# Two PSUM banks for the gate products, and one block's lookups written behind the second half's norm

## The chip, the cores and the metric

The kernel runs on one core of a Trainium2 chip. The metric is the device time of one execution in microseconds (us). The median of the runs of the kernel before is 4191.13 us. Profiles come from one execution that the hardware profiler recorded; its times are counted from the start of its span.

## What is computed

One layer of a diffusion backbone over 1024 tokens with 1024 channels: token mixers (two linear-attention scans in both directions, merged by gates and followed by an output projection), then a PEER expert feed-forward, then a final normalisation. The change touches the border of the two and the first part of PEER:

```python
x = x + mod[2] * mixer_output(...)                 # output projection w_out, residual
h = modulate(rmsnorm(x, norm_ffn_g), shift, scale) # norm before PEER
q = h @ wq                                         # 8 heads x 2 x 128
v1, i1 = top_k(q1 @ k1.T, 16); v2, i2 = top_k(q2 @ k2.T, 16)
top_s, top_c = top_k(v1[:, None] + v2[None, :], 16)   # 16 experts per head, 128 per token
expert = i1[top_c // 16] * 128 + i2[top_c % 16]       # the lookups
gate = softmax(top_s)
out = sum_e gate[e] * gelu(u[e] . h) * v[e]           # 16384 experts
```

## The kernel before, in words

The 1024 tokens are 8 blocks of 128. The mixers work on two halves of 4 blocks. After them comes, per half, `merge_step` (branch projections, 8 steps), `out_proj` (the output projection, one 128-row tile `xt` per block, two PSUM products `pso` each) and `next_norm` (row statistics on ACT, scaling on DVE at L84 through `norm_T`, transposes on PE into `pt_m`, and the normalised halves `hb`).

While the second half is merged and projected, the first half already chooses its experts. A generator `first()` yields after each piece: `choosing(0, pp)` (scores and top-16 of 8 heads, nine pieces per head) and then `route(n)` for blocks 0, 1 and 2. `route` is the lookup step: it turns the chosen candidate numbers into the two key numbers and the softmax weights (`sel`), almost all on DVE (tiles `abur`, `abfr`, `eqr`, `selr`, L801 to L840). `CS = (9, 1, 1)` says how many pieces are taken from the generator at each merge step, after each projected tile, and in the norm. 8 merge steps times 9 exhaust `choosing`; the projected tiles 0, 1 and 2 then take `route` of blocks 0, 1 and 2, the fourth finds the generator empty, and so does the norm.

PEER is evaluated in two ways. Blocks 0, 1 and 4 gather their expert rows one by one (`gathering`: an indirect DMA issued by POOL at L1000, six rows in flight; a DVE instruction at L979 for rows of `peer_u`, at L984 for rows of `peer_v`). Blocks 2, 3, 5, 6 and 7 go densely over all 16384 experts in 128 tiles of 128, and need a dense gate matrix per block. `gate_block` builds it for four tokens at a time: two DVE instructions make one-hot vectors `oh` (L1068, which the profile names L89, and L1069; four buffers), eight PE matmuls add them up in PSUM as `pgm` (L1070 to L1073), and one ACT instruction evicts the bank into `gs` (L1074), which goes to DRAM after 8 such steps (L1076). There are 160 steps: 64 for blocks 2 and 3, 96 for blocks 5, 6 and 7.

```python
pgm = ppg.tile([P, TB, P], F32, name=f"pgm{n}_{c0}", tag="go")
for t in range(TB):
    for j in (2, 3):
        PE.matmul(pgm[:, t, :], lhsT=oh[:, 0, :, t], rhs=oh[:, j, :, t], start=j == 2, stop=j == 3)
S.activation(gs[:, :, t0:t0 + TB].rearrange("p i n -> p n i"), pgm, AF.Copy, scale=SA / SG)
```

Between the gate steps `early_tile` runs the first product of 75 expert tiles: eight PE transposes of the loaded rows into `put` (L1021), ACT copies the high half into `uT` (L1024) and a full copy into `uf` (L1026), POOL subtracts them for the low half of `uT` (L1027), and 48 matmuls accumulate into `ph` (L100 in `mm3`), which ACT evicts with Gelu into `ac` (L1039). A counter of estimated costs (`U_US`, `G_E`, the numbers that the generators yield) says how many such tiles and gathers are written between the gate steps; the change leaves those numbers as they are. Between blocks 3 and 5 stands `choosing(1)`, the choice for the second half.

PSUM has 8 banks of 2 KB per partition. In this part `put` holds two, the two halves of `ph` one each, `pgm`, the transposes `tr` and the scores `q` one each: seven.

The program text is not the order on the engines. A scheduling layer takes the recorded instructions and lays out one queue per engine, moving an instruction ahead of others written before it where its inputs allow; each engine then runs its queue strictly in order.

Of the kernel before, what the change touches and what calls it, by code (L numbers as in the profile page):

```python
# [8 lines left out]
F32 = mybir.dt.float32  # L9
# [9 lines left out]
P = 128  # L19
# [25 lines left out]
TB = 4  # L45
# [12 lines left out]

U_US = 6.5
G_E = 4.2  # L60
CS = (9, 1, 1)
FILL = (0, 0, 2, 0, 0, 1, 1, 0)
AHEAD = 6
PRE = 0.25
# [3 lines left out]
def tile_layer(ctx: ExitStack, tc: tile.TileContext, x, c, ctxt, c_ctx, ada_w, ada_b, norm_mix_g,  # L68
# [19 lines left out]
    def tt(eng, out, in0, in1, op):  # L88
        eng.tensor_tensor(out=out, in0=in0, in1=in1, op=op)  # L89
# [6 lines left out]
    def mm3(ps, lh, ll, rh, rl, nk=KC):  # L96
        n, last = 0, 3 * nk - 1
        for k in range(nk):
            for a, b in ((lh, rh), (lh, rl), (ll, rh)):
                PE.matmul(ps, lhsT=a(k), rhs=b(k), start=n == 0, stop=n == last)  # L100
                n += 1
# [39 lines left out]
    def rms_cols(tiles, pl, tag):  # L141

        n = len(tiles)
        ss = pl.tile([P, n], F32, name=f"ss_{tag}", tag="ss", bufs=3)
        for i, t in enumerate(tiles):
            sq = pl.tile([P, D], F32, name=f"sq_{tag}{i}", tag="sq")
            S.activation(sq, t, AF.Square, accum_out=ss[:, i:i + 1])
        S.activation(ss, ss, AF.Ln, scale=1.0 / D, bias=eps)
        S.activation(ss, ss, AF.Exp, scale=-0.5)
        return ss  # L150

    def norm_T(tiles, ss, dst, sc, sh, pl, pp, tag, rows_of=None):

        for i, t in enumerate(tiles):
            tsc(V, t, t, ss[:, i:i + 1], ALU.mult)
        w = len(tiles) * P
        for k in range(KC):
            pt = pp.tile([P, 512], F32, name=f"pt_{tag}{k}", tag="pt", bufs=2)
            for i, t in enumerate(tiles):
                PE.transpose(pt[:, i * P:(i + 1) * P], t[:, k * P:(k + 1) * P], ident)  # L160
            hi = dst(0, k)
            S.activation(hi, pt[:, :w], AF.Identity, scale=sc(k), bias=sh(k))
            yt = pl.tile([P, 512], F32, name=f"yt_{tag}{k}", tag="yt", bufs=2)
            tsc(V, yt[:, :w], pt[:, :w], sc(k), ALU.mult, sh(k), ALU.add)
            tt(G, dst(1, k), yt[:, :w], hi, ALU.subtract)
            if rows_of is not None:
                rows_of(k, yt)
# [5 lines left out]
    with ExitStack() as mixers:  # L173
# [704 lines left out]
        def out_proj(hf, yT, fill=None):  # L878
            tiles = []
            for i in range(4):  # L880
                n = hf * 4 + i
                xt = mg.tile([P, D], F32, name=f"xr{n}", tag="xr", bufs=4)
                ld(out=xt, in_=x[n * P:(n + 1) * P, :])
                for h2 in range(2):
                    cs = slice(h2 * 512, (h2 + 1) * 512)
                    ps = pp.tile([P, 512], F32, name=f"pso{n}_{h2}", tag="pj", bufs=2)
                    mm3(ps, lambda k: yT[:, k, 0, i * P:(i + 1) * P], lambda k: yT[:, k, 1, i * P:(i + 1) * P],
                        lambda k: wo[:, 0, k, cs], lambda k: wo[:, 1, k, cs])
                    tm = mg.tile([P, 512], F32, name=f"tm{n}_{h2}", tag="tm")
                    tt(V, tm, ps, mod2[:, cs], ALU.mult)  # L890
                    tt(G, xt[:, cs], xt[:, cs], tm, ALU.add)
                st_(out=x1_d[n * P:(n + 1) * P, :], in_=xt)
                tiles.append(xt)
                if fill is not None:
                    for _ in range(CS[1]):
                        next(fill, None)
            return tiles

        def h2_rows(hf):

            own = [n - hf * 4 for n in GB if n // 4 == hf]
            o = sum(n // 4 < hf for n in GB)

            def rows_of(k, yt):
                pt = pp.tile([P, 512], F32, name=f"ptr{hf}_{k}", tag="tr")
                w = len(own)
                for i, b in enumerate(own):
                    PE.transpose(pt[:, i * P:(i + 1) * P], yt[:, b * P:(b + 1) * P], ident)
                hn = mg.tile([P, 2, P], F32, name=f"hn{hf}_{k}", tag="hn", bufs=2)
                S.activation(hn[:, 0:w], pt[:, 0:w * P].rearrange("p (a b) -> p a b", a=w), AF.Copy, scale=1.0 / SH2)  # L910
                st_(out=h2_d[o:o + w, :, k * P:(k + 1) * P].rearrange("a p b -> p a b"), in_=hn[:, 0:w])

            return rows_of

        def next_norm(hf, tiles, fill=None):
            ss = rms_cols(tiles, mg, f"x1_{hf}")
            if fill is not None:
                for _ in range(CS[2]):
                    next(fill, None)
            norm_T(tiles, ss, lambda s, k: hb[hf][:, s, k, :], lambda k: cols2[:, 1, k:k + 1], lambda k: cols2[:, 0, k:k + 1],  # L920
                   mg, pp, f"m{hf}_", h2_rows(hf))

        yin = load_y(0)
        yT = mg.tile([P, KC, 2, HT], F16, name="yT0", tag="yT")
# [6 lines left out]
        yT = mg.tile([P, KC, 2, HT], F16, name="yT1", tag="yT")  # L931
# [8 lines left out]

        first_half = first()
        for j in range(KC):
            for _ in range(CS[0]):
                next(first_half, None)
            merge_step(1, j, yin, yT)
        next_norm(1, out_proj(1, yT, first_half), first_half)
        for _ in first_half:
            pass
        if "x1" in dbg:
# [94 lines left out]
    with ExitStack() as st:  # L1044
        pg = pool(st, "pg", reuse_waits="tile")
        ppg = pool(st, "ppg", space=PSUM, reuse_waits="tile")
# [14 lines left out]
        def gate_block(rT, n, nb):  # L1061

            gs = pg.tile([P, P, NB], F32, name=f"gs{n}_{nb}", tag="gs", bufs=2)
            for t0 in range(0, NB, TB):
                c0 = nb * NB + t0
                oh = pg.tile([P, 4, P, TB], F16, name=f"oh{n}_{c0}", tag="oh", bufs=4)
                cols_ = lambda j: rT[:, j:j + 2, c0:c0 + TB].unsqueeze(2).to_broadcast([P, 2, P, TB])
                tt(V, oh[:, 0:2], iota.unsqueeze(1).to_broadcast([P, 2, P, TB]), cols_(0), ALU.is_equal)  # L1068
                vmark[0] = V.tensor_tensor(out=oh[:, 2:4], in0=oh[:, 1:2].to_broadcast([P, 2, P, TB]), in1=cols_(2), op=ALU.mult)  # L1069
                pgm = ppg.tile([P, TB, P], F32, name=f"pgm{n}_{c0}", tag="go")  # L1070
                for t in range(TB):
                    for j in (2, 3):
                        PE.matmul(pgm[:, t, :], lhsT=oh[:, 0, :, t], rhs=oh[:, j, :, t], start=j == 2, stop=j == 3)  # L1073
                S.activation(gs[:, :, t0:t0 + TB].rearrange("p i n -> p n i"), pgm, AF.Copy, scale=SA / SG)  # L1074
                yield 1.65
            st_(out=G_d[DB.index(n) * (P // NB) + nb], in_=gs)  # L1076
# [196 lines left out]
```

## Time and profile before

| | |
|---|---|
| median of 3 runs | 4191.13 us (4185.23 to 4202.76) |
| the profiled execution's own time | 4186.54 us |
| its span | 4184.8 us |
| PE busy | 3875.4 us, 93% |
| DVE busy | 2961.0 us, 71% |
| POOL busy | 1624.5 us, 39% |
| ACT busy | 1417.9 us, 34% |
| DMA, mean over the span | 211 GB/s |
| gate products (L1073), first to last start | 1902.2 to 2824.3 us |

Busy shares are averages over stages with different limits, so the rows below are cut by stage: the border to PEER (1860 to 1900 us), the gates of blocks 2 and 3 (1900 to 2140), the choice of the second half without any gate step (2140 to 2440), and the gates of blocks 5, 6 and 7 (2440 to 2826). "Idle" of an engine in such a stretch is the stretch less its busy time.

### The profile page before, as it was taken

The numbers are of one execution on the slowest core, as the hardware profiler recorded it, in microseconds if no ns is written. First come the engines' busy times: TensorE is split into PE (matmuls) and PEld (weight loads), VectorE is DVE, ScalarE is ACT, GpSimd is POOL, SyncE is SP. The second block draws the span as 40 slices with busy tenths as digits, with TensorE's granted clock in tenths as the row PEclk, the third lists the DMA queues.
The fourth block names the chain that finished last, engine by engine and source line by source line (L and its number), as shares of the span: only waits on it lengthen the run. The fifth ranks groups of instructions, "written<-read, shape, count | busy, mean of one in ns | idle before, by whom it ended". The sixth has DMA issues, their size and how long they took to land.

```text
span 4184.8 us, 60506 instructions
## 1 busy us (share of the span) xinstructions
PE 3875.4 (93%) x23802; PEld 2352.4 (56%) x23802; DVE 2961.0 (71%) x5292; ACT 1417.9 (34%) x2186; POOL 1624.5 (39%) x1197
## 2 busy tenths in 40 slices
PE   6999999999999999978999988897999999999997
PEld 2665666656565444436766656675555554554553
DVE  5345446343546513688889899995889898889999
ACT  5335344242333202115532344553222222222222
POOL 2111111010111002016666577765555465555553
PEclk8999999999999999999999999999999999999999
DMA  5222122221323573317887778898999998988997
GB/s 191 73 79 86 46 81 82 63 85 46 91 71 108 162 261 125 116 57 270 328 309 276 248 254 314 307 335 310 310 316 321 314 318 308 323 289 304 319 309 247
DMA packets 435308, 884.66 MB, mean 211 GB/s; under 512 B 28512, under 2 KB 245067, under 8 KB 431439
## 3 DMA queue, kind: packets, MB, share of 16 engines
q0 software_dynamic: 110592, 402.70, 27.7%
q1 hardware_dynamic: 202676, 320.19, 22.8%
q10 hardware_dynamic: 121754, 157.89, 10.8%
q8 instruction: 187, 3.06, 0.3%
q14 instruction: 99, 0.80, 0.1%
HBM read 764.80 MB, written 115.88 MB: 210 GB/s over the span
## 4 chain that ended last, share of the span: by engine, by line
PE 39%; DVE 30%; DMA 10%; issue 10%; ACT 5%; POOL 4%; SPq 0%; ACTq 0%; DVEq 0%; POOLq 0%
DVE gacc L984 7%; DVE row_False L979 4%; PE ph L100 4%; DMA acr<-act_d 3%; DMA row_False<-in_peer_u_dram,idx 3%; PE pj_f0h L100 3%; PE pv_g L100 3%; PE pv_h L100 2%; PE pgm L1073 2%; PE pj_f1h L100 2%; PE pj_m L100 2%; DVE acc L1168 2%; POOL row_False L1000 2%; DVE v L94 2%; PE pq L100 2%
## 5 line engine op out<-in xcount | busy, mean ns | idle before, releaser
L100 PE MATMUL ph<-hb,uT 128*128 128x256 f16 (+1 forms) x6144 | 905.1, 304 | 44.6 <-POOL uT L1027 33.6
L100 PE MATMUL pe<-v,w 128*128 128x512 f16 x3840 | 864.2, 385 | 70.2 <-DVE acc L1168 65.4
L100 PEld LDWEIGHTS <-uT 128*128 128x128 f16 x6144 | 614.0, 100 | 271.1 <-POOL uT L1027 37.4
L100 PEld LDWEIGHTS <-w 128*128 128x128 f16 x3840 | 380.5, 99 | 541.1 <-issue 105.2
L1000 POOL DMA_INDIRECT row_True<-in_peer_v_dram,idx x384 | 482.3, 1256 | 360.2 <-DVE gacc L984 293.4
L1000 POOL DMA_INDIRECT row_False<-in_peer_u_dram,idx x384 | 504.8, 1315 | 267.8 <-DVE row_False L979 174.0
L979 DVE SCALAR_TENSOR_TENSOR row_False<-row_False,h2n 128x1024 f32<-128x1024 f32 x384 | 520.9, 1389 | 70.1 <-DMA row_False<-in_peer_u_dram,idx 60.2
L984 DVE SCALAR_TENSOR_TENSOR gacc<-row_True,dots,gacc 128x1024 f32<-128x1024 f32 x381 | 535.0, 1404 | 22.6 <-DMA row_True<-in_peer_v_dram,idx 21.1
L1027 POOL TENSOR_TENSOR uT<-uf,uT 128x512 f16<-128x512 f32 x256 | 379.3, 1494 | 200.3 <-ACT uf L1026 197.9
L93 ACT ACTIVATE v<-vn 128x1024 f16<-128x1024 f32 x128 | 135.1, 1056 | 495.4 <-DMA vn<-in_peer_v_dram 368.6
L1074 ACT ACTIVATE gs<-pgm 128x512 f32<-128x512 f32 x160 | 171.8, 1074 | 167.2 <-PE pgm L1073 160.1
L94 DVE SCALAR_TENSOR_TENSOR v<-vn,v 128x1024 f16<-128x1024 f32 x128 | 176.5, 1380 | 54.2 <-ACT v L93 54.2
L1073 PE MATMUL pgm<-oh 128*128 128x128 f16 x1280 | 176.7, 295 | 40.4 <-ACT gs L1074 26.3
L1039 ACT ACTIVATE ac<-ph 128x256 f32<-128x256 f32 (+1 forms) x256 | 109.6, 440 | 289.6 <-PE ph L100 258.3
L1168 DVE TENSOR_TENSOR acc<-pe,acc 128x512 f32<-128x512 f32 x310 | 206.6, 683 | 0.8 <-PE pe L100 0.8
L100 PE MATMUL pj_m<-hb,w_m 128*128 128x512 f16 x768 | 182.3, 393 | 2.3 <-DVE lf_g L86 1.6
L1073 PEld LDWEIGHTS <-oh 128*128 128x128 f16 x1280 | 144.9, 116 | 67.6 <-issue 45.5
L100 PE MATMUL pq<-hb,w_wq 128*128 128x512 f16 x768 | 177.1, 384 | 1.0 <-POOL hb L89 0.7
L1024 ACT ACTIVATE uT<-put 128x512 f16<-128x512 f32 x256 | 153.7, 600 | 69.0 <-PE put L1021 61.6
L1026 ACT ACTIVATE uf<-put 128x512 f32<-128x512 f32 x256 | 155.1, 606 | 25.5 <-POOL uT L1027 25.1
L100 PEld LDWEIGHTS <-hb 128*128 128x128 f16 x1536 | 150.3, 98 | 17.7 <-issue 0.3
L89 POOL TENSOR_TENSOR lf_g<-lf_g,ab_g 128x1280 f32<-128x1280 f32 x8 | 23.1, 2890 | 336.3 <-ACT ab_g L639 336.3
(364 smaller groups left out, 5649.8 us busy)
## 6 DMA issues: line engine op xcount, KB each, us to landing
un<-in_peer_u_dram SPq DMA_DIRECT2D x128, 512.0 KB
vn<-in_peer_v_dram SPq DMA_DIRECT2D x128, 512.0 KB
G_d<-gs ACTq DMA_DIRECT2D x20, 2048.0 KB
gt<-G_d ACTq DMA_DIRECT2D x32, 1280.0 KB
act_d<-ac ACTq DMA_DIRECT2D x80, 320.0 KB
acr<-act_d SPq DMA_DIRECT2D x80, 320.0 KB
mw<-in_ada_w_dram SPq DMA_DIRECT2D x32, 512.0 KB
w_wq<-wq_d SPq DMA_DIRECT2D x32, 512.0 KB
```

The costliest lines, as they stand in the source:

```text
L93: S.activation(hi, src, AF.Copy, scale=float(scale))
L94: return V.scalar_tensor_tensor(out=lo, in0=src, scalar=float(scale), in1=hi, op0=ALU.mult, op1=ALU.subtract)
L100: PE.matmul(ps, lhsT=a(k), rhs=b(k), start=n == 0, stop=n == last)
L979: V.scalar_tensor_tensor(out=row, in0=row, scalar=1.0, in1=h2n, op0=ALU.mult, op1=ALU.mult, accum_out=dots[:, s:s + 1])
L984: V.scalar_tensor_tensor(out=gacc[n], in0=row, scalar=dots[:, s:s + 1], in1=gacc[n], op0=ALU.mult, op1=ALU.add)
L1000: G.indirect_dma_start(out=row, out_offset=None, in_=src[0], in_offset=bass.IndirectOffsetOnAxis(ap=gsel[n][0][:, s:s + 1], axis=0))
L1024: S.activation(hi, pv, AF.Copy, scale=SU)
L1026: S.activation(uf, pv, AF.Copy, scale=SU)
L1027: pace[0] = G.tensor_tensor(out=lo, in0=uf, in1=hi, op=ALU.subtract)
L1073: PE.matmul(pgm[:, t, :], lhsT=oh[:, 0, :, t], rhs=oh[:, j, :, t], start=j == 2, stop=j == 3)
L1074: S.activation(gs[:, :, t0:t0 + TB].rearrange("p i n -> p n i"), pgm, AF.Copy, scale=SA / SG)
L1168: vmark[0] = V.tensor_tensor(out=acc[n][:, hs], in0=ps, in1=acc[n][:, hs], op=ALU.add)
```

## The change

`pgm` gets two PSUM banks instead of one. In `out_proj` the generator is advanced only after the first two tiles, so that `route` of block 2 is written behind `next_norm(1, ...)`, in the loop that empties the generator; the argument of `next_norm` that found it empty is gone.

```diff
-CS = (9, 1, 1)
+CS = 9
...
-                if fill is not None:
-                    for _ in range(CS[1]):
-                        next(fill, None)
+                if fill is not None and i < 2:
+                    next(fill, None)
...
-        def next_norm(hf, tiles, fill=None):
+        def next_norm(hf, tiles):
             ss = rms_cols(tiles, mg, f"x1_{hf}")
-            if fill is not None:
-                for _ in range(CS[2]):
-                    next(fill, None)
...
-            for _ in range(CS[0]):
+            for _ in range(CS):
                 next(first_half, None)
             merge_step(1, j, yin, yT)
-        next_norm(1, out_proj(1, yT, first_half), first_half)
+        next_norm(1, out_proj(1, yT, first_half))
         for _ in first_half:
             pass
...
-                pgm = ppg.tile([P, TB, P], F32, name=f"pgm{n}_{c0}", tag="go")
+                pgm = ppg.tile([P, TB, P], F32, name=f"pgm{n}_{c0}", tag="go", bufs=2)
```

What it does to the queues shows at two places. The first is DVE's queue in `out_proj`, where the third projected tile `tm_0` of block 6 is multiplied; `abur`, `t1r` and `abfr` belong to block 2's lookups, `eqr_1` and the first `selr` to block 1's. Before:

```order
L806 TENSOR_SCALAR abur_14319<-ti_12357 128x128
L89 TENSOR_TENSOR eqr_1_14246<-eqr_1_14246,idf_12358 128x2048
L807 TENSOR_SCALAR abur_14319<-ti_12357 128x128
L89 TENSOR_TENSOR eqr_1_14246<-eqr_1_14246 128x8x128
L89 TENSOR_TENSOR tm_0_14286<-pso_0_14261,mod_11395 128x512
L89 TENSOR_TENSOR eqr_1_14246<-eqr_1_14246 128x8x64
L86 TENSOR_SCALAR t1r_14323<-ti_12357 128x128
```

In the change:

```order
L806 TENSOR_SCALAR abur_14505<-ti_12357 128x128
L89 TENSOR_TENSOR eqr_1_14246<-eqr_1_14246,idf_12358 128x2048
L807 TENSOR_SCALAR abur_14505<-ti_12357 128x128
L89 TENSOR_TENSOR eqr_1_14246<-eqr_1_14246 128x8x128
L89 TENSOR_TENSOR tm_0_14286<-pso_0_14261,mod_11395 128x512
L89 TENSOR_TENSOR eqr_1_14246<-eqr_1_14246 128x8x64
L86 TENSOR_SCALAR t1r_14509<-ti_12357 128x128
```

Only the running numbers of block 2's tiles differ (14319 and 14505): they are recorded later and stand at the same place of the queue. With the numbers taken off, the queues of DVE, ACT, POOL and PE are the same, row by row, from the start of the program up to the first gate steps, and SP's queue is the same to the end. A kernel with the first part of the change alone has, on all five engines, the queues of the kernel before.

The second place is PE's queue in the gates of block 2, around four gate steps (tokens 80 to 95; `put` are the transposes of the next expert tile, `ph_12` the products of the present one). A line of dots stands for more rows of the same kind. Before:

```order
L1073 MATMUL pgm_80_15510<-oh_80_15507 128x128
...
L1021 MATMUL put_0_15562<-ident,un_15559 128x128 x4
L1021 MATMUL put_1_15571<-ident,un_15559 128x128 x4
...
L100 MATMUL ph_12_15581<-hb_85,uT_15422 128x256
...
L1073 MATMUL pgm_84_15523<-oh_84_15520 128x128
...
L100 MATMUL ph_12_15581<-hb_85,uT_15422 128x256
...
L1073 MATMUL pgm_88_15536<-oh_88_15533 128x128
...
L100 MATMUL ph_12_15581<-hb_85,uT_15422 128x256
...
L1073 MATMUL pgm_92_15549<-oh_92_15546 128x128
```

In the change (four lines fewer ahead of them, so L1073 is L1069 and L1021 is L1017):

```order
L1069 MATMUL pgm_80_15510<-oh_80_15507 128x128
...
L1069 MATMUL pgm_84_15523<-oh_84_15520 128x128
...
L1017 MATMUL put_0_15562<-ident,un_15559 128x128 x4
L1017 MATMUL put_1_15571<-ident,un_15559 128x128 x4
...
L100 MATMUL ph_12_15581<-hb_85,uT_15422 128x256
...
L1069 MATMUL pgm_88_15536<-oh_88_15533 128x128
...
L1069 MATMUL pgm_92_15549<-oh_92_15546 128x128
```

Before, 6, 8 and 7 matmuls of `ph_12` stand between the four gate steps, and 27 behind the last; now the steps come in pairs, with the transposes and 2 matmuls of `ph_12` between the pairs and 46 behind the second. Up to the 64th gate step PE's queue holds 864 matmuls of `ph` before and now, so no expert tile has moved from one stage to another; at the very end, 34 of them followed the last gate step and 46 do now. ACT's queue at the same place was, before:

```order
L1074 ACTIVATE gs_2_15367<-pgm_80_15510 128x4x128
L1024 ACTIVATE uT_15561<-put_0_15562 128x512
L1026 ACTIVATE uf_0_15568<-put_0_15562 128x512
L1074 ACTIVATE gs_2_15367<-pgm_84_15523 128x4x128
L1024 ACTIVATE uT_15561<-put_1_15571 128x512
L1026 ACTIVATE uf_1_15577<-put_1_15571 128x512
L1074 ACTIVATE gs_2_15367<-pgm_88_15536 128x4x128
L1074 ACTIVATE gs_2_15367<-pgm_92_15549 128x4x128
```

and is in the change:

```order
L1070 ACTIVATE gs_2_15367<-pgm_80_15510 128x4x128
L1070 ACTIVATE gs_2_15367<-pgm_84_15523 128x4x128
L1020 ACTIVATE uT_15561<-put_0_15562 128x512
L1070 ACTIVATE gs_2_15367<-pgm_88_15536 128x4x128
L1070 ACTIVATE gs_2_15367<-pgm_92_15549 128x4x128
L1022 ACTIVATE uf_0_15568<-put_0_15562 128x512
L1020 ACTIVATE uT_15561<-put_1_15571 128x512
L1022 ACTIVATE uf_1_15577<-put_1_15571 128x512
```

The evictions `gs` also pair up, and the last copy `uf_1`, which POOL needs for the low half of the next tile, stands behind two more evictions than before.

## Rows read from the trace of the kernel before

**Rows 1.** The page, part 1: busy us (share) and instructions.
```profile
PE 3875.4 (93%) x23802; PEld 2352.4 (56%) x23802; DVE 2961.0 (71%) x5292; ACT 1417.9 (34%) x2186; POOL 1624.5 (39%) x1197
```
**Rows 2.** The page, part 5: count | busy, mean ns | idle before, releaser.
```profile
L1074 ACT ACTIVATE gs<-pgm 128x512 f32<-128x512 f32 x160 | 171.8, 1074 | 167.2 <-PE pgm L1073 160.1
L1073 PE MATMUL pgm<-oh 128*128 128x128 f16 x1280 | 176.7, 295 | 40.4 <-ACT gs L1074 26.3
```
**Rows 3.** Windows by stage: PE, PEld, DVE, ACT, POOL busy; PEclk, DMA share, GB/s.
```profile
1860.00:1900.00 40.00, 18.96 (x72) 10.97 (x71) 28.47 (x48) 13.07 (x25) 13.30 (x11) 0.62 0.21 71
1900.00:2140.00 240.00, 225.83 (x1708) 179.46 (x1707) 205.67 (x346) 128.66 (x198) 164.14 (x123) 1.00 0.86 319
2140.00:2440.00 300.00, 272.35 (x1786) 181.04 (x1784) 265.53 (x901) 90.55 (x175) 193.44 (x156) 0.98 0.78 268
2440.00:2690.00 250.00, 216.40 (x1533) 165.95 (x1532) 249.09 (x300) 118.53 (x185) 189.30 (x126) 0.93 0.82 289
2690.00:2826.00 136.00, 124.85 (x951) 101.34 (x950) 126.99 (x186) 75.41 (x109) 92.26 (x68) 0.99 0.93 336
```
**Rows 4.** Waits of PE, 1860 to 1880 us: total us, times, longest.
```profile
PE pt_m L160 <- DVE xr L84: 14.0, 1, 14.0
```
**Rows 5.** Timeline, 2056 to 2062 us: start, us, instruction [idle before <- releaser].
```profile
2055.71 1.28 DVE L1069 TENSOR_TENSOR oh<-oh,rTr 128x1024 f16<-128x1024 f16 x2
...
2058.47 1.11 PE L1073 MATMUL pgm<-oh 128*128 128x128 f16 x8 [0.17 <-ACT gs L1074]
...
2059.40 1.00 PE L100 MATMUL ph<-hb,uT 128*128 128x384 f16 x5
2059.61 1.07 ACT L1074 ACTIVATE gs<-pgm 128x512 f32<-128x512 f32 x1 [0.29 <-PE pgm L1073]
...
2060.73 1.10 PE L1073 MATMUL pgm<-oh 128*128 128x128 f16 x8 [0.34 <-ACT gs L1074]
```
**Rows 6.** Waits of PE, 1900 to 2140 us.
```profile
PE pgm L1073 <- ACT gs L1074: 11.5, 31, 0.6
PE pgm L1073 <- DVE oh L1069: 1.9, 3, 1.4
```
**Rows 7.** Waits of DVE, 1900 to 2140 us.
```profile
DVE row_False L979 <- DMA row_False<-in_peer_u_dram,idx: 15.9, 10, 4.0
DVE oh L89 <- PE pgm L1073: 9.1, 6, 2.3
...
DVE oh L89 <- ACT gs L1074: 2.0, 1, 2.0
```
**Rows 8.** Waits of PE, 2440 to 2690 us.
```profile
PE ph L100 <- POOL uT L1027: 14.3, 5, 4.8
PE pgm L1073 <- DVE oh L1069: 6.9, 5, 3.2
PE pgm L1073 <- ACT gs L1074: 6.9, 19, 0.5
```
**Rows 9.** Waits of PE, 2690 to 2826 us.
```profile
PE pgm L1073 <- ACT gs L1074: 8.4, 22, 0.5
```
**Rows 10.** Waits of DVE, 2690 to 2826 us.
```profile
DVE row_False L979 <- DMA row_False<-in_peer_u_dram,idx: 4.5, 7, 1.5
```
**Rows 11.** Timeline, 2817 to 2834 us, the end of the gates.
```profile
2817.73 0.69 DVE L1069 TENSOR_TENSOR oh<-oh,rTr 128x1024 f16<-128x1024 f16 x1
...
2823.55 1.10 PE L1073 MATMUL pgm<-oh 128*128 128x128 f16 x8 [0.27 <-ACT gs L1074]
...
2824.47 5.17 PE L100 MATMUL ph<-hb,uT 128*128 128x256 f16 x34
...
2824.68 1.07 ACT L1074 ACTIVATE gs<-pgm 128x512 f32<-128x512 f32 x1 [0.27 <-PE pgm L1073]
...
2831.91 0.85 SPq L1152 DMA_DIRECT2D vn<-in_peer_v_dram  x2
```

## The prediction

> **What bounds the kernel now.** I read the page first, then the busy time by stage, then in each stage the waits of the two engines that are nearly full, and last the timeline at two places. On the page PE is busy for 93% of the span and DVE for 71% [rows 1], which says little about a stage. The row of the edited instruction says more: PE was idle for 26.3 us in all because a gate step's matmuls found their only PSUM bank not yet evicted, and ACT, which evicts it in 1074 ns, was idle for 160.1 us waiting for PE [rows 2]. So ACT is not short of time; the single bank makes two engines take turns. The timeline shows the turn: matmuls start at 2058.47, the eviction runs from 2059.61 for 1.07 us, and the next matmuls start at 2060.73 after 0.34 us of idle PE; five matmuls of an expert tile fill most of the gap [rows 5]. That filler is why a full turn costs PE some 0.4 us and not over a microsecond.
>
> What such a wait is worth depends on the stage [rows 3]:
> - 1900 to 2140 us (gates of blocks 2 and 3): PE is busy 225.83 of 240 us, DVE 205.67. PE's idle time is 14.2 us, of which 11.5 are the eviction, in 31 waits [rows 6]. DVE has 34.3 us to spare, and 11.1 of its waits are for one-hot buffers that PE or ACT hold back [rows 7]. PE is the bound and the eviction its main leak.
> - 2140 to 2440 us: there is no gate step, so nothing there is edited.
> - 2440 to 2690 us: DVE is busy 249.09 of 250 us. PE is idle for 33.6 us there and waits 6.9 for evictions [rows 8], but DVE ends the stage whatever PE does.
> - 2690 to 2826 us: both are nearly full, PE idle 11.2 us, 8.4 of them for evictions [rows 9], DVE idle 9.0, half of it for gathered rows [rows 10].
>
> **The change, part by part.** *The lookups.* As written, they leave the projection, where DVE is in the way of the norm: PE stands 14.0 us until DVE scales the rows [rows 4]. But the rows of DVE's queue ahead of this text are the same before and now, the lookups of block 2 included, and so are the other engines' up to the first gate steps. What is recorded later is laid back to its old place. No instruction and no DMA of this part moves past anything on any queue, SP's and POOL's included. Cost and gain: 0 us, by the queues and not by an overlap, so there is no cover to lose.
>
> *The second bank.* Nothing is added or removed: 160 steps, the same matmuls, evictions and DMAs. What goes is the turn-taking, and the queues of PE and ACT show pairs of steps. Stage by stage:
> - 1900 to 2140: the 11.5 us of [rows 6] go. A pair needs two one-hot tiles. Two DVE instructions take 1.28 us [rows 5], so the second tile is ready 0.64 us after the first where DVE makes them together, 1.28 where one after the other. With DVE ahead of PE in most of the stage (its 9.1 us of waits for PE's buffers, against 1.9 us of PE's waits for one-hots) I charge two delays of 1.28, 2.6 us. Term: -9. Bounds: -11.5 if no pair waits; on the other side, if every one of the 32 pairs waited 1.28 us, +41.0 - 11.5 = +29.5. I take the value near the lower end because [rows 7] has DVE waiting for PE and not the reverse.
> - 2440 to 2690: 0, since DVE has 0.9 us of idle time in 250. Bound: -6.9.
> - 2690 to 2826: at most the 8.4 us, and no more than the 9.0 that DVE can give. DVE's last one-hot is ready at 2818.42 (2817.73 plus 0.69), the last gate matmuls start only at 2823.55 and their eviction ends at 2825.75 [rows 11]: 7.3 us for work whose bare chain is 1.10 plus 1.07. Against it, 46 instead of 34 expert matmuls now stand between the last gate step and the next transposes, which release the loads of the following stage; at 5.17/34 us each [rows 11] that is 1.8 us. I take half of the 8.4: -4, between 0 and -8.4.
> - Behind it: the gate matrix is stored, loaded again, and the first `vn` load issued at 2831.91 [rows 11]; all of that follows the end of the gates and shifts with it. DMA moves 319 to 336 GB/s here [rows 3] whichever way PE is ordered.
>
> Sum: -9 + 0 - 4 = **-13 us**, with ends at -26.8 (11.5 + 6.9 + 8.4) and 0 before the rivals. The profiled execution took 4186.54 us, so 4173.5; the median shown, 4191.13, lies 4.6 above that execution, so I forecast **4178 us**. What is late next: the one-hot tiles in the first stage, the gathered rows in the last.
>
> One rule speaks against a second bank. First the rows: the granted clock is 1.00, the 2.4 GHz level, from 1900 to 2140 with all of its 31 short waits, and 0.62 in the 40 us around PE's 14.0 us stop [rows 3, 4]; only the long stop is seen with a lower clock. The Trainium skill, "TensorE: Matmul & The Clock Gate", section "A second HAM failure mode: psum-queue depth-cycling", tells of a kernel that cycled through PSUM banks in each iteration, idled PE briefly between groups of matmuls, and had its clock swing between both levels. By that rule the pairs would lose the full clock; this trace does not bear it out for waits of up to 0.6 us.
>
> **The rivals.**
> 1. *Nothing to be had* (0 us, 4191). PE's saved time comes back as waits for one-hots, for gathered rows or for POOL's low halves. For it: DVE waits 15.9 us for gathered rows in the first stage [rows 7], and a row that comes no sooner holds the one-hots queued behind it; DVE is full in the second [rows 3]. Against: POOL, which issues those gathers, is busy only 164 of 240 us and itself waits for copies that PE's transposes feed. Chance 0.22.
> 2. *Both engines loosen* (-26 us, 4165; at most 26.8 plus the 9.1 us of DVE's waits for PE, -36, 4155). The whole 26.3 of [rows 2] becomes time, the DVE-bound stretch too, since a smoother PE also feeds ACT and POOL evenly. Against: 249.09 busy of 250. Chance 0.13.
> 3. *Slower: the second one-hot of each pair.* PE's queue is strict; a pair placed ahead of 46 matmuls of an expert tile blocks them when the second tile is late. Price: 32 pairs at 1.28 us in the first stage, +29.5 net, 4221. It decides when DVE is less than two tiles ahead of PE. Against: [rows 6, 7]; for: 6.9 us of such waits in 2440 to 2690 already [rows 8]. Chance 0.06.
> 4. *Slower: the copies behind the evictions.* `uf_1` stands two evictions later in ACT's queue, 2 x 1.07 us, so POOL's low half of the next tile comes later; PE already waits 14.3 us for it in one stretch [rows 8]. If each of the 20 sets of 8 steps lost the full 2.14 us: +43 - 26 = +17, 4208. Against: 46 matmuls at 0.15 us, 7 us, stand as cover where it was some 4. Chance 0.06.
> 5. *The clock.* If the 240 us of the first stage were granted 0.93, as 2440 to 2690 is [rows 3], 225.83 x (1/0.93 - 1) = +17, less the 13: 4195. It is the mechanism that the rule above would have. Chance 0.03.
>
> That the change does not do what it says is certain for its first half, by the queues; it is in every case above.
>
> **How the numbers follow.** The forecast has the remaining 0.50: its own range is 4170 (half of the way to rival 2's end) to 4188. A measurement of this kernel tells about 0.5%, 21 us, from no change; so faster means below 4170, slower above 4212. Faster: rival 2 (0.13) and 0.05 of the forecast's lower edge, 0.18. Slower: rival 3 (0.06), and 0.02 of rival 4, 0.08. The same: 0.74. For 8 in 10 the range goes from 4155, rival 2's end, to 4206: it takes in the forecast, rivals 1, 2 and 5 and leaves out most of 3 and 4 and some scatter, the shown runs alone spreading from 4185 to 4203.
>
> **What would show it.** Right: PE's waits for evictions at the gate lines fall from 26.3 us to under 3; PE's idle time from 1900 to 2140 falls to under 6 us, and the last gate step of block 3 comes some 9 us sooner; from 2440 to 2690 DVE stays full; the border at 1860 to 1900 still has its 14.0 us. Wrong: PE's waits for `oh` or for POOL's `uT` grow by as much as the evictions fell (rivals 1, 3, 4), the granted clock of the first stage drops below 1.00 (rival 5), or the time between the stages changes although no instruction there moved.

## The result, and the profile after

The change is slower: 4218.04 us median of 6 runs (4215.25 to 4220.15) against 4185.09 us for the kernel before on the same chip (6 runs, 4184.27 to 4202.76), a ratio of the means of 1.0069 with a 95% interval of 1.0053 to 1.0086. The forecast was 4178 us in a range of 4155 to 4206. The profiled execution of the change took 4216.42 us, its span 4214.7; the span before was 4184.8.

The page of the change, parts 1 and 5; these answer to [rows 1, 2], with two more groups, DVE's use of the gathered rows and POOL's low halves:

```profile
PE 3882.2 (92%) x23802; PEld 2356.1 (56%) x23802; DVE 2954.4 (70%) x5292; ACT 1416.5 (34%) x2186; POOL 1617.5 (38%) x1197
...
L975 DVE SCALAR_TENSOR_TENSOR row_False<-row_False,h2n 128x1024 f32<-128x1024 f32 x384 | 509.6, 1353 | 122.8 <-DMA row_False<-in_peer_u_dram,idx 120.2
...
L1023 POOL TENSOR_TENSOR uT<-uf,uT 128x512 f16<-128x512 f32 x256 | 378.7, 1494 | 228.1 <-ACT uf L1022 225.7
...
L1070 ACT ACTIVATE gs<-pgm 128x512 f32<-128x512 f32 x160 | 170.0, 1090 | 152.5 <-PE pgm L1069 147.2
L1069 PE MATMUL pgm<-oh 128*128 128x128 f16 x1280 | 172.6, 296 | 49.4 <-DVE oh L1065 49.3
```

The eviction waits of PE that the change was about are gone. In their place the same matmuls wait for one-hots, and longer: 49.3 us against 26.3 [rows 2]. Two groups of the kernel before say where to look:

```profile
L979 DVE SCALAR_TENSOR_TENSOR row_False<-row_False,h2n 128x1024 f32<-128x1024 f32 x384 | 520.9, 1389 | 70.1 <-DMA row_False<-in_peer_u_dram,idx 60.2
...
L1027 POOL TENSOR_TENSOR uT<-uf,uT 128x512 f16<-128x512 f32 x256 | 379.3, 1494 | 200.3 <-ACT uf L1026 197.9
```

DVE's waits for gathered rows doubled, from 60.2 to 120.2 us, and POOL waits 28 us more for the copies `uf` that feed its low halves. The busy time by stage of the change, as in [rows 3]:

```profile
1860.00:1900.00 40.00, 18.95 (x73) 11.26 (x72) 28.45 (x48) 13.07 (x25) 13.30 (x11) 0.62 0.20 66
1900.00:2140.00 240.00, 217.84 (x1625) 174.23 (x1624) 192.76 (x293) 122.97 (x188) 152.38 (x116) 0.94 0.80 302
2140.00:2440.00 300.00, 275.40 (x1804) 183.51 (x1802) 259.59 (x938) 91.17 (x178) 192.20 (x157) 0.97 0.78 270
2440.00:2690.00 250.00, 211.62 (x1505) 162.58 (x1506) 249.80 (x297) 115.42 (x181) 187.41 (x127) 0.92 0.82 289
2690.00:2826.00 136.00, 121.53 (x937) 98.62 (x936) 122.50 (x181) 73.90 (x107) 84.98 (x66) 0.97 0.86 323
```

The border at 1860 is untouched. From 1900 to 2140 all engines do less than before, PE and DVE both: PE's idle time went from 14.2 to 22.2 us, the granted clock from 1.00 to 0.94, the DMA share from 0.86 to 0.80. No engine took over as the bound; they wait for each other. The waits of PE, DVE and POOL in that stage, which answer to [rows 6, 7]:

```profile
POOL uT L1023 <- ACT uf L1022: 65.9, 17, 9.6
...
DVE row_False L975 <- DMA row_False<-in_peer_u_dram,idx: 43.3, 18, 8.2
...
PE pgm L1069 <- DVE oh L1065: 21.8, 11, 4.5
...
PE ph L100 <- POOL uT L1023: 0.2, 1, 0.2
```

DVE's waits for PE's one-hot buffers, 9.1 us in [rows 7], are no longer listed: DVE has gone from ahead of PE to behind it. The 21.8 us of one-hot waits are 14.9 at the second step of a pair (7 waits), 4.6 at the first (3) and 2.3 at a step by itself.

DVE's queue is another one too, which the queues read ahead of the prediction did not cover. Up to the 64th gate step it holds 128 one-hot instructions. Before, rows were mostly used four at a time behind the one-hots of four steps, and 22 of the 128 stood directly behind the use of a row. In the change, uses of rows stand between the one-hots, and 41 do; e1 and e2 below, counted the same way in their traces, give 22 and 41 again.

The timeline of the change shows one turn of what happened (start, us, instruction, [idle before <- releaser]):

```profile
2026.04 1.22 DVE L975 SCALAR_TENSOR_TENSOR row_False<-row_False,h2n 128x1024 f32<-128x1024 f32 x1 [5.19 <-DMA row_False<-in_peer_u_dram,idx]
...
2027.19 0.69 DVE L89 TENSOR_TENSOR oh<-iota,rTr 128x1024 f16<-128x1024 f16 x1
...
2028.84 1.23 DVE L975 SCALAR_TENSOR_TENSOR row_False<-row_False,h2n 128x1024 f32<-128x1024 f32 x1 [0.96 <-DMA row_False<-in_peer_u_dram,idx]
...
2029.99 0.69 DVE L1065 TENSOR_TENSOR oh<-oh,rTr 128x1024 f16<-128x1024 f16 x1
...
2030.73 1.11 PE L1069 MATMUL pgm<-oh 128*128 128x128 f16 x8 [4.20 <-DVE oh L1065]
...
2032.54 1.12 PE L1069 MATMUL pgm<-oh 128*128 128x128 f16 x8 [0.69 <-DVE oh L1065]
...
2033.47 1.04 PE L1017 MATMUL put<-ident,un 128*128 128x128 f32 x4
...
2037.67 1.11 ACT L1070 ACTIVATE gs<-pgm 128x512 f32<-128x512 f32 x1 [2.90 <-PE pgm L1069]
...
2038.57 0.65 ACT L1020 ACTIVATE uT<-put 128x512 f16<-128x512 f32 x1
...
2040.36 0.63 ACT L1022 ACTIVATE uf<-put 128x512 f32<-128x512 f32 x1
...
2041.07 3.69 POOL L1023 TENSOR_TENSOR uT<-uf,uT 128x512 f16<-128x512 f32 x2 [9.58 <-ACT uf L1022]
...
2044.91 1.76 POOL L996 DMA_INDIRECT row_False<-in_peer_u_dram,idx  x1 [0.15 <-issue]
...
2046.97 1.97 POOL L996 DMA_INDIRECT row_False<-in_peer_u_dram,idx  x1 [0.30 <-issue]
...
2059.35 1.23 DVE L975 SCALAR_TENSOR_TENSOR row_False<-row_False,h2n 128x1024 f32<-128x1024 f32 x1 [7.28 <-DMA row_False<-in_peer_u_dram,idx]
...
2061.25 1.00 PE L1069 MATMUL pgm<-oh 128*128 128x128 f16 x7 [4.46 <-DVE oh L1065]
```

Read it from the top. A row lands late. A one-hot takes two DVE instructions, and the second one, at 2029.99, stands in DVE's strict queue behind the use of a row. PE waits 4.20 us for it and then runs the pair; only then come the transposes of the next tile. ACT reaches their copies at 2038.57, behind a third step's eviction for which it waits 2.90 us. POOL has waited 9.58 us for `uf`, and the gathers stand behind its low halves: they issue at 2044.91 and 2046.97. The second of them is the row that DVE waits for, 7.28 us, at 2059.35; the next one-hot stands behind it, and PE waits 4.46, this time at the second step of a pair. This is theory R, the ring: row, one-hot, pair, transposes, copies, low halves, gathers, row.

### The profile page after: what moved, and what is told of

It reads as the page before. It is cut to its first block, busy times and chain, and to the rows that moved or that the text cites. A ratio compares the mean times of both kernels' runs of the same rounds, so it can differ in the third digit from the quotient of the medians.

```text
span 4214.7 us, 60536 instructions
## 1 busy us (share of the span) xinstructions
PE 3882.2 (92%) x23802; PEld 2356.1 (56%) x23802; DVE 2954.4 (70%) x5292; ACT 1416.5 (34%) x2186; POOL 1617.5 (38%) x1197
## 4 chain that ended last, share of the span: by engine, by line
PE 40%; DVE 28%; issue 12%; DMA 11%; POOL 5%; ACT 4%; SPq 0%; ACTq 0%; DVEq 0%; POOLq 0%
DVE gacc L980 8%; DMA row_False<-in_peer_u_dram,idx 4%; PE ph L100 4%; DVE row_False L975 3%; PE pe L100 3%; DMA acr<-act_d 3%; PE pj_f0h L100 3%; PE pv_g L100 2%; PE pj_m L100 2%; PE pv_h L100 2%; PE pq L100 2%; PE pj_f1h L100 2%; POOL row_False L996 2%; PE pj_qh L100 2%; DVE eqr L89 2%
## 5 line engine op out<-in xcount | busy, mean ns | idle before, releaser
L996 POOL DMA_INDIRECT row_False<-in_peer_u_dram,idx x384 | 494.6, 1288 | 283.3 <-DVE row_False L975 181.3
L975 DVE SCALAR_TENSOR_TENSOR row_False<-row_False,h2n 128x1024 f32<-128x1024 f32 x384 | 509.6, 1353 | 122.8 <-DMA row_False<-in_peer_u_dram,idx 120.2
L1069 PE MATMUL pgm<-oh 128*128 128x128 f16 x1280 | 172.6, 296 | 49.4 <-DVE oh L1065 49.3
L1069 PEld LDWEIGHTS <-oh 128*128 128x128 f16 x1280 | 142.8, 117 | 68.7 <-DVE oh L1065 55.0
L1022 ACT ACTIVATE uf<-put 128x512 f32<-128x512 f32 x256 | 155.4, 607 | 26.6 <-POOL uT L1023 26.4
L1017 PE MATMUL put<-ident,un 128*128 128x128 f32 x1024 | 143.7, 282 | 14.7 <-ACT uf L1022 14.7
```

The source lines that it names most:

```text
L975: V.scalar_tensor_tensor(out=row, in0=row, scalar=1.0, in1=h2n, op0=ALU.mult, op1=ALU.mult, accum_out=dots[:, s:s + 1])
L996: G.indirect_dma_start(out=row, out_offset=None, in_=src[0], in_offset=bass.IndirectOffsetOnAxis(ap=gsel[n][0][:, s:s + 1], axis=0))
L1017: PE.transpose(pt[:, k * P:(k + 1) * P], un[:, (q * 4 + k) * P:(q * 4 + k + 1) * P], ident)
L1022: S.activation(uf, pv, AF.Copy, scale=SU)
```

## The experiments

The rivals were B (a second bank costs something of its own), P (a pair costs by itself, because its second one-hot is waited for) and L (the lookups' move costs the time). All ratios are against the kernel before on the same chip, with 95% intervals.

**Each half alone.** First the lookups' half of the diff, then the bank's (`bufs=2` for `go`).

> The first half of the change alone: the lookups behind the norm, one bank for the gate products. Its queues on all five engines read the same as those of the kernel before. Theory R (the ring: steps in pairs put the next tile's transposes, their evictions, the low halves on POOL and the gathers behind them, behind a one-hot that waits for a gathered row) and theory B (a second bank costs something of its own): 4185 us, ratio 0.998 to 1.002. Theory L (the lookups' move costs the time, by another state of the engines at the start of the gates): about 4218 us, ratio 1.007.

> The second half of the change alone: two banks, the lookups where they were. R and B: the whole loss, about 4218 us, ratio 1.005 to 1.009, with gate evictions waits of TensorE at 0 and its one-hot waits near 49 us. L: 4160 to 4185 us, not slower than before.

Measured: 4189.17 us, ratio 0.9995 (0.9987 to 1.0004), for the lookups; 4220.09 us, ratio 1.0070 (1.0054 to 1.0087), for the bank. L falls: the bank makes the whole loss, with one-hot waits of 21.1 us and row waits of 43.9 from 1900 to 2140.

**Two banks, steps one by one.** An order edge (no wait) from each eviction to the next step's first matmul:

```diff
-                        PE.matmul(pgm[:, t, :], lhsT=oh[:, 0, :, t], rhs=oh[:, j, :, t], start=j == 2, stop=j == 3)
+                        mm = PE.matmul(pgm[:, t, :], lhsT=oh[:, 0, :, t], rhs=oh[:, j, :, t], start=j == 2, stop=j == 3)
+                        if t == 0 and j == 2 and evict[0] is not None:
+                            tc.add_manual_dep(mm.ins, evict[0].ins.name,
+                                              mybir.DependencyInfo(mybir.DependencyClass.NoSync, mybir.DependencyReason.DATA),
+                                              reason="step_after_evict")
-                S.activation(gs[:, :, t0:t0 + TB].rearrange("p i n -> p n i"), pgm, AF.Copy, scale=SA / SG)
+                evict[0] = S.activation(gs[:, :, t0:t0 + TB].rearrange("p i n -> p n i"), pgm, AF.Copy, scale=SA / SG)
```

> Two banks as in the change, but each gate step is queued on TensorE only after the eviction of the step before has been queued (an order, not a wait), so that steps stand one by one again with the transposes of the next tile behind the first step of a tile, not behind the second. R: the loss is gone, and with the eviction waits gone too it is no slower than before: 4165 to 4188 us, ratio 0.995 to 1.001; waits of POOL for the second copy of a tile (uf) back near those of before (198 us), DVE's waits for gathered rows near 60 us. B: the loss stays, 4210 to 4225 us.

Measured: 4206.98 us, 1.0043 (1.0028 to 1.0058): between the two. The edge did not restore the old order: in block 3 every second tile's transposes still stood behind two steps after a run of 47 products (step, 47 products, step, step, part of the transposes, step, the rest). In the first stage row waits were 38.9 us, POOL's waits for `uf` 71.0 and PE's waits for one-hots 20.3, though no step stood directly behind another. My expectation was wrong about what the edge does; the steps still stand close, so the run alone decides nothing between R and P.

**Transposes early.** The next tile's transposes are written behind the first of a tile's steps:

```diff
+            if 1.6 < t_ < U_US and not turned and pend is not None:
+                turn_next()
             while t_ >= U_US and pend is not None:
```

> Two banks, and the next tile's transposes written behind the first gate step of a tile instead of behind all four; TensorE's queue has then a step, the 8 transposes, and the other steps partly one by one. R: most of the loss is gone, 4180 to 4200 us, ratio 0.999 to 1.004, POOL's waits for uf under 215 us. B: 4210 to 4225 us. A theory P (the pair itself costs, because the second one-hot of a pair is waited for, whatever stands behind it) expects a part of the loss to stay, since some steps here still stand close: 4195 to 4210 us, with one-hot waits still over 40 us.

Measured: 4188.89 us, 0.9997 (0.9985 to 1.0008). The loss is gone with two banks in place, so B falls. POOL runs its low halves and gathers in the same order as in the change up to 2600 us. Not the transposes alone have moved, though: of the change's 25 pairs up to the 64th step, PE still runs 6. The waits from 1900 to 2140:

```profile
PE pgm L1069 <- DVE oh L1065: 8.7, 8, 3.1
...
DVE row_False L975 <- DMA row_False<-in_peer_u_dram,idx: 30.0, 18, 5.6
...
POOL uT L1023 <- ACT uf L1022: 32.6, 14, 9.8
```

**The reverse: transposes late.** They are queued behind the last of a tile's steps, with two banks (e9) and, with no second bank at all, in the kernel before (e10):

```diff
-            uTn = u_turn(pend, u_load(pend)) if pend is not None else None
+            if pend is not None:
+                un = u_load(pend)
+                with tc.issue_after(steps[-1].ins) if len(steps) >= 1 else ExitStack():
+                    uTn = u_turn(pend, un)
```

> The change with the next tile's transposes queued behind the last of a tile's four gate steps instead of behind the second, the pairs kept as they are. R: the path from a late row to the next rows gets longer, so the loss grows: 4222 to 4260 us, ratio 1.008 to 1.018, waits for gathered rows between 1900 and 2140 over the change's 43 us. P (the pairs by themselves): the time of the change, 4213 to 4222 us. If the last transposes find a product run that fills the time, and the path does not matter, it is at most the change's time.

> One bank, as before, and only the transposes moved: behind the last of a tile's four gate steps, which stand one by one with products between. R: slower than before without any second bank, 4200 to 4240 us, ratio 1.004 to 1.013, waits for gathered rows and one-hots up. P and B: the time of before within 5 us, ratio 0.999 to 1.001.

Measured: e9 4234.95 us, 1.0106 (1.0091 to 1.0120); e10 4229.33 us, 1.0098 (1.0084 to 1.0113). One bank, one step at a time, and there is a loss all the same, for which neither P nor B accounts. In e10 the waits from 1900 to 2140 read

```profile
PE pgm L1069 <- DVE oh L1065: 5.0, 4, 1.8
...
DVE row_False L975 <- DMA row_False<-in_peer_u_dram,idx: 29.6, 12, 6.2
...
POOL uT L1023 <- ACT uf L1022: 63.3, 16, 9.3
```

and from 2440 to 2690 (14.3 and 6.9 in [rows 8])

```profile
PE ph L100 <- POOL uT L1023: 23.5, 14, 4.8
PE pgm L1069 <- DVE oh L1065: 13.7, 4, 8.9
```

So late transposes lose as much as the change, but not in the same place. By the start of its eviction the 65th gate step, at 2480 before, is 9.2 us late in e10 and 12.8 in the change; the 113th, at 2679, is 28.9 us late in e10 and 11.8 in the change. Some 20 us of e10's loss come where the change loses nothing, and PE's waits for low halves grow there more than those for one-hots. One detail missed: in the first stage e9's row waits are 35.5 us, not over the change's 43.3, and its one-hot waits 17.5, not over 21.8, though over the whole span the row waits are the same (123.4 and 120.2). What e9 loses beyond the change is not traced to these waits.

**The link cut on POOL.** Between the gate steps the gathers are no longer queued behind the newest low halves:

```diff
-                    with tc.issue_after(pace[0].ins):
+                    with tc.issue_after(pace[0].ins) if gates_done[0] else ExitStack():
                         G.indirect_dma_start(out=row, out_offset=None, in_=src[0],
...
```

> The change, with the gathers between the gate steps no longer queued on POOL behind the newest low halves (TensorE's queue stays as in the change, pairs first and transposes behind them; POOL's queue is left to the scheduler, which puts some gathers ahead of the low halves). R: the link from the late transposes to the late rows is cut, so DVE's waits for gathered rows between 1900 and 2140 fall from 43 us towards the 16 of before, TensorE's one-hot waits there from 22 to under 12, and the time to 4180 to 4200 us, ratio 0.998 to 1.004. P (the pair by itself): 4205 to 4222 us, one-hot waits as in the change.

Measured: 4233.12 us, 1.0094 (1.0074 to 1.0114), slower still, so the time was misjudged. The waits from 1900 to 2140 say why:

```profile
PE ph L100 <- POOL uT L1023: 18.3, 8, 6.1
PE pgm L1069 <- DVE oh L1065: 0.9, 1, 0.9
...
DVE row_False L975 <- DMA row_False<-in_peer_u_dram,idx: 19.6, 10, 8.0
...
POOL row_False L996 <- DVE row_False L975: 50.3, 20, 5.0
```

One-hot waits fell from 21.8 to 0.9 us and row waits from 43.3 to 19.6, with all 25 pairs still in PE's queue. That is as R says, and against P. It need not be the work of the cut link alone: in this run DVE's queue has the one-hots of four steps together ahead of the rows again, and only 15 of 128 one-hot instructions stand behind a row's use. But now gathers that wait for a free row buffer stand ahead of the low halves, and PE waits 18.3 us for those where it waited 0.2. One strict queue serves both, and the two orders trade one wait for the other.

**No gathers between the gates.** `G_E = 0.0`, with two banks and with one:

> The change without any gather between the gate steps (all 768 gathers of the two blocks that are computed by gathering move into the last stage, the same number in all). Both kernels of this pair lose the cover for the gathers, so only their difference counts. R: without rows on DVE there is no ring, and two banks are not slower than one: the last gate eviction comes 0 to 20 us earlier than in the one-bank kernel beside it, and the time is equal or less, by 0 to 20 us. B: two banks are slower here too, by 15 to 33 us.

> The same without gathers between the gate steps, one bank for the gate products. R: the last gate eviction 0 to 20 us later than with two banks, the time equal or more by 0 to 20 us. B: faster than with two banks by 15 to 33 us.

Measured: 4450.06 us (1.0612, 1.0590 to 1.0634) with two banks, 4487.31 us (1.0694, 1.0669 to 1.0719) with one. Without rows in the ring two banks are 37 us *faster*, more than I expected. The last gate eviction starts at 2717.18 us:

```profile
2717.18 1.05 ACT L1070 ACTIVATE gs<-pgm 128x512 f32<-128x512 f32 x1 [0.53 <-PE pgm L1069]
```

and with one bank at 2759.06:

```profile
2759.06 1.06 ACT L1070 ACTIVATE gs<-pgm 128x512 f32<-128x512 f32 x1 [0.28 <-PE pgm L1069]
```

In e7 the first 64 steps stand in the same 25 pairs, and no one-hot wait of PE is listed from 1900 to 2140: here P falls, as the whole cause. The second bank does what it says when no gathered rows stand in DVE's queue; it is the rows that turn it into a loss.

**Even steps.** The tile's work in four pieces: step, transposes, 12 products, step, 12 products, step and so on.

```diff
+            while t_ >= U_US / 4 and parts is not None:
+                t_ -= U_US / 4
...
+                    gathers(G_E / 4)
```

> Two banks, and the tile's work written in four pieces between the gate steps, so that TensorE's queue reads step, transposes, 12 products, step, 12 products and so on. R: transposes stand behind one step each, so not slower than with the transposes early: 4170 to 4192 us, ratio 0.996 to 1.001; whether the even spacing gains beyond that R leaves open. P: the only form here with no steps close together, so it expects the best time of all, under 4180 us, ratio under 0.998. If rows that come late for any reason set the pace, the time is that of before within 5 us.

> Two banks, the even steps, and 4.6 instead of 4.2 gathers for each tile between the gate steps. The two kernels without early gathers show what a gather is worth: against the kernel with the transposes early, 312 gathers moved cost the last stage some 370 us and save the gates some 105 us, so one more early gather is worth up to 0.85 us. 0.4 more for each tile over the some 75 tiles are 30 gathers: if the gates take them at that price, up to 25 us faster, 4165 us, ratio 0.994. If the rows' transfers are the limit between the gates already (a DMA share of 0.89 between 1900 and 2140), nothing is gained: ratio 0.998 to 1.003. R has no third answer, but a tighter ring could also cost 5 to 15 us.

> The same with 5.0 gathers for each tile: some 60 gathers more between the gates. Where early gathers are worth 0.85 us each, up to 50 us faster; where the transfers are the limit, the same as with 4.6 or worse: ratio 0.999 to 1.01.

Measured: e6 4188.91 us, 0.9998 (0.9986 to 1.0010); with more gathers e11 4194.61 us, 1.0014 (1.0005 to 1.0023), and e12 4202.30 us, 1.0036 (1.0024 to 1.0048). P's best case is no faster than before. More early gathers don't pay: in e11 PE's one-hot waits in the first stage rise again to 18.2 us.

**Where e6's gain went.** In e4 and e6 the products run 7 to 11 us ahead of the kernel before near 2110 to 2160 us, about the 9 us of my first term; by 2240 they do not. Waits of e6 from 2140 to 2240:

```profile
POOL idf L786 <- DVE ii L762: 31.8, 2, 16.2
...
PE ph L1117 <- POOL uT L1023: 16.7, 2, 11.5
```

Before, these two are 13.5 and 4.6 us. A cast of 0.31 us (`idf`, line 786) waits in POOL's queue for DVE's ids, with the low halves behind it. Moved to DVE, with even steps (e13), in the kernel before (e14) and in the change (e15):

```diff
-                G.tensor_copy(out=idf[:, :, :, h, :], in_=ii)
+                V.tensor_copy(out=idf[:, :, :, h, :], in_=ii)
```

> Even steps, two banks, and the cast of a head's ids (line 786, 312 ns on POOL, 8 times beside the gates) done by DVE right behind the ids, so that POOL's low halves and gathers no longer stand behind a wait for DVE. If the gates' gain is given back at that cast: TensorE's waits for low halves between 2140 and 2240 fall from 16.7 to under 8 us and the time to 4168 to 4182 us, ratio 0.995 to 0.999. If it is given back because rows or DVE set the pace there anyway, the wait only changes its name: ratio 0.999 to 1.002.

> The kernel before with the cast on DVE. There TensorE waits only 4.6 us for low halves between 2140 and 2240, but 24.1 us from 2140 to 2440: if the cast holds POOL, 0 to 15 us faster, ratio 0.996 to 1.000; if rows or DVE set the pace, ratio 0.999 to 1.002.

> The change with the cast on DVE. Its loss arises before 2100 us, before the first of the eight casts beside the gates matters, so R keeps it: slower than the kernel before with the cast on DVE by 20 to 35 us. A theory that the cast makes the loss expects it gone.

Measured: e13 4167.85 us, 0.9952 (0.9939 to 0.9966); e14 4166.34 us, 0.9948 (0.9935 to 0.9962); e15 4191.90 us, 1.0006 (0.9996 to 1.0017), 25.6 us behind e14. In e14, from 1900 and from 2140 us on:

```profile
1900.00:2140.00 240.00, 225.53 (x1705) 178.89 (x1702) 203.55 (x344) 128.36 (x197) 160.71 (x122) 1.00 0.86 317
2140.00:2440.00 300.00, 288.23 (x1929) 194.54 (x1926) 274.94 (x959) 99.61 (x195) 204.23 (x160) 0.99 0.82 288
```

The first stage is that of [rows 3]; in the second PE does 288.23 us of work where it did 272.35. The cast was worth about 0.5%, with one bank as with two, and the change's loss stays beside it. e14, the kernel before with that one line moved, beats both kernels here.

**What else the edits moved.** Counted in the traces up to the 64th gate step; the one-hot waits are those of PE from 1900 to 2140, in us.

| run | steps directly behind another | one-hot instructions directly behind a row's use, of 128 | one-hot waits | ratio |
|---|---|---|---|---|
| before | 0 | 22 | 1.9 | |
| the change | 25 | 41 | 21.8 | 1.0069 |
| e3 | 0 | 39 | 20.3 | 1.0043 |
| e4, transposes early | 6 | 22 | 8.7 | 0.9997 |
| e5, link cut on POOL | 25 | 15 | 0.9 | 1.0094 |
| e6, even steps | 1 | 57 | 9.1 | 0.9998 |
| e9, transposes last | 25 | 44 | 17.5 | 1.0106 |
| e10, the same, one bank | 0 | 49 | 5.0 | 1.0098 |

A rival that I did not test is DVE's new order, in which a one-hot stands behind a row more often. By itself it does not make the loss, since e6 has more of it and loses nothing. But e4 takes away the late transposes, most pairs and this order together, and e10's edit brings the order with it. The nearest to the transposes alone is e10 against e6: both are without pairs and have rows between the one-hots, and they differ in the transposes, the bank and the spacing of the products. No run moves the transposes with DVE's queue held. So it is shown that the second bank loses by the order that it brings (e2, e4, e6) and only with gathered rows (e7); that the late transposes, and not DVE's order with them, carry the ring is argued from the runs together.

## Why the prediction was wrong

- *The lookups, 0 us*: right (e1).
- *Eviction waits from 26.3 us to under 3*: right, none is left. The step that failed is the other half of the first term, "two late one-hots of 1.28 us" for -9 us in the first stage. PE waits 21.8 us for one-hots there, 11 times, up to 4.5 us each, and the last gate step of block 3 comes 8.3 us later, not some 9 sooner. I took 1.28 us as the most that a one-hot can be late, because that is what DVE needs for two; but a one-hot is as late as the row whose use stands ahead of it on DVE, and that row depends on PE's own queue. I had taken [rows 7] to say that DVE stays ahead; its queue in the gates, which the change reorders, I had not read.
- *What is moved*: I read the new order as pairs and priced the second step of a pair. I did not price the 8 transposes that the pair pushes back from behind one step to behind two. PE needs their result a tile later, so they looked free; POOL's gathers, queued behind their low halves, need them at once. With the transposes early, later still, and late without a second bank (e4, e9, e10) the loss goes, grows and appears; in each of them other rows of the queues move too.
- *Rival 3* had the sign, at 4221 us nearly the time, and the place of 14.9 of the 21.8 us, the second step of a pair. Its size was luck: not 32 delays of 1.28 us but 7 of 2.1 on average, since what a step waits for is a row, and without rows the same pairs cost nothing (e7). *Rival 4* named one true link, the copies behind evictions on ACT, and priced it where it costs little in the change: PE waits 0.2 us for low halves in the first stage. *Rival 1* came nearest in words ("a row that comes no sooner holds the one-hots queued behind it"), but I let it stop at zero; rows came later, and the ring closes on itself.
- *The clock, rival 5*: the granted clock did fall, to 0.94, but it went with the long waits: from 2030 to 2050, right behind the first long wait of the timeline, and from 2050 to 2070, around the second, it is 0.85 and 0.83, from 2070 to 2090 1.00, the 2.4 GHz level. The Trainium skill, "TensorE: Matmul & The Clock Gate", section "A second HAM failure mode: psum-queue depth-cycling", tells of a kernel that cycled through PSUM banks, idled PE briefly but often between groups of matmuls, and had its clock swing. The runs do not bear out the cycling as the cause here: e4 and e6 cycle through the same two banks at 0.99, with one-hot waits of up to 3.1 and 2.3 us instead of 4.5. I wrote that only the long stop is seen with a lower clock; [rows 3, 8] had 0.93 too, from 2440 to 2690 with waits of up to 4.8 us. The clock added to the loss: PE's idle time grew by 8 us, while its recorded instructions fell from 1708 to 1625, 4.9% of 240 us or about 12 us of work, an estimate.
- *2440 to 2690, 0 us*: right, DVE is busy 249.80 of 250.
- *The end of the gates, -4 us*: wrong; the last gate eviction, at 2824.68 in [rows 11], starts 11.1 us later:

```profile
2835.82 1.09 ACT L1070 ACTIVATE gs<-pgm 128x512 f32<-128x512 f32 x1 [0.49 <-PE pgm L1069]
...
2849.68 0.38 ACTq L1198 DMA_DIRECT2D gt<-G_d  x1
...
2868.08 0.82 DVE L89 TENSOR_TENSOR acr<-acr,gt 128x640 f32<-128x640 f32 x1 [8.56 <-DMA gt<-G_d]
```

I wrote that all behind the gates "shifts with it". It shifts by more. Before:

```profile
2833.57 0.38 ACTq L1202 DMA_DIRECT2D gt<-G_d  x1
...
2850.51 0.83 DVE L89 TENSOR_TENSOR acr<-acr,gt 128x640 f32<-128x640 f32 x1 [2.63 <-DMA gt<-G_d]
```

The load of the gates `gt` issues 16.1 us later and DVE waits 8.56 us for it instead of 2.63, so the first use is 17.6 us late. Nor did DMA keep its 319 to 336 GB/s "whichever way PE is ordered": it moves 302 from 1900 to 2140 and 323 from 2690 to 2826. In sum: the 64th gate step is 8.3 us late, the 65th 12.8, the last 11.1; the thirteenth use of the gates, at 3054 before, is 25.9 us late, and the end of the span 29.9. So the border behind the gates adds about 13 and the final stage some 5. Those last 5 are not the change: e1, whose queues are those of the kernel before, loses as much there in its profiled execution. Why the border adds 13 was not tried by itself; in e4 and e6, where the gates end on time, it adds at most some 4.

## What to carry to other kernels

When an edit lets a scheduler hoist work on one strict queue, list what it was hoisted over, and follow that work's results to every queue that they gate, not only back to the same engine: here it was a transpose that nobody on PE needed soon. Read the new order of every queue, DVE's here too. Before counting on a wait that disappears, look for a ring of queues through the place that it leaves. And a small instruction that waits for another engine at the head of a busy queue can be worth more than it takes: moving casts of 0.31 us from POOL to DVE brought 23 us, where the edit of this document was forecast to bring 13.

## What the runs showed that I had not expected

Two banks saved 37 us in the kernel without early gathers, more than all of the 26.6 us that PE waited for evictions there with one bank: the wait that the profile shows is not the most that its removal can give. The last gate eviction comes 41.9 us sooner. From 1900 us up to it PE is idle 14.9 us with two banks and 41.4 with one, and busy 802.1 and 817.6 for 5931 and 5948 recorded matmuls: 26.5 us of the gain is idle time, the rest busy time of nearly the same work. Why that work is busy for less is not shown. And waits of a few microseconds in PE's queue went with a lower granted clock in the same stage (0.94 in the change and in e9, 0.97 in e10, against 0.99 to 1.00 before and in e4 and e6), which thirty-one waits of 0.4 us on average [rows 6] had not done.
